# A hybrid streaming encoder step: key loads spread over the query tiles, and split weights kept in DRAM for the second token group

## The chip, the cores and the metric

The kernel runs on one core of one Trainium2 chip. The metric is the device time of one execution in microseconds (us); the figure for the kernel before is the median of three runs. A profile is one more execution, with the hardware profiler on. Names of engines: TensorE (PE in the rows; PEld is its weight load), VectorE (DVE), ScalarE (ACT), GpSimd (POOL), SyncE (SP). A name with a q at its end (SPq, ACTq, POOLq) is the engine's queue of instructions, where it issues DMAs.

## The reference, cut to what matters

One layer: RMSNorm, one input projection to `[q | k | v | z_a | forget | B | C | h_c | z_c]`, forgetting attention (8 heads of 64) beside a short gated convolution, one output projection, residual, final norm. 16 meta tokens and 2048 prompt tokens make 2064 positions; 128 sample tokens (8 streams of 16, each with 256 cached rows) go through the same weights.

```python
h = rmsnorm(xp, norm_g[l])
q, k, v, za, logf, bg, u, zc = project(h, w_in[l], b_f[l])     # p = h @ w_in, 1024 x 4104
o_a = fox_prompt_attention(q, k, v, logf)                      # softmax(q.k/8 + c_t - c_s, causal) @ v
y_c = bg * causal_conv(u_full, conv_w[l])
cat = concat([o_a * silu(za), y_c * silu(zc)])
xp = xp + cat @ w_out[l]
```

All values are float32. The matrix engine gets each operand as two halves: `h` is the value rounded to the short format (F32R), `l` the difference, and a product is `h*h + l*h + h*l`, three matmuls.

## The kernel before

**Token groups.** The positions are worked through in two groups (`GROUPS`, line 39): the first has 1280 positions and the 128 sample tokens, 1408 columns in four tiles (256, 384, 384, 384); the second has the other 784, in tiles of 256, 256 and 272. Each group goes through norm, values of heads 0 to 3, then keys, queries and gates of the four pairs of heads woven with attention, then the convolutions. Between the groups stand the sample attention and the splitting of the output weights `w_out` (`split_out`), woven with the first group's convolutions; the output projection comes last.

**Weights.** A block of input weights is 1024 x 128, `raw`, [128, 8, 128] in float32, 0.52 MB, read in pieces of 512 bytes. `weight_order` (line 535) lists the 30 blocks of one group, twice. Two of the 30 make up the values of heads 4 to 7; 28 are split singly, 56 in both groups. `fetch_w` (line 465) issues the load of the next block on ScalarE's queue into the one buffer `raw`; `split_w` (line 474) copies it to `wh` on ScalarE, subtracts on VectorE into `wl`, and fetches the next. `wh` and `wl` have two buffers each. `load_w` (line 517) hands a block to its user and splits the one after it. `project` (line 544) does the matmuls: per token tile 8 x 3 of them into one PSUM tile `ps`, of which there are two. `split_wv` (line 492) does the same for 256 columns of values, with the subtraction on GpSimd (`wvh`, `wvl`); for heads 0 to 3 the forget columns are added (`raw8`).

**What a projection leaves.** Keys and queries are split (`eh`, `el`, two buffers each) and stored on GpSimd's queue (`STORES`, line 1563) to DRAM: `kh_d`, `kl_d`, `qh_d`, `ql_d`, for sample tokens `sqk_d`; gates and convolution results from `kf` (two buffers) to `gz_d` and `cat_d`.

**Attention.** A unit is 256 queries of one head (272 in the last), two or three score tiles: 5 units a head in the first group, 3 (7 tiles) in the second. `scores_of` (line 966) loads, scores and exponentiates; `weights_of` transposes and splits the weights (`tp`, `ph`, `pl`); `values_of` multiplies with the values `vb` (one buffer, loaded per head). `load_head` (line 905) loads a head's keys into one of two sets of buffers: two halves for `ka`, the upper half once more for `kb` (64 rows of up to 2064 positions, 0.53 MB each in the second group), and the sums of the forget gates. `load_queries` does the like for a unit (`qa`, `qb`). All of this is issued on SP. At each unit `scores_of` first loads the keys of the next head, if they are not yet asked for, then the queries of the next unit:

```python
            for ahead in range(2):
                if loaded < H and loaded <= h + ahead and ("k", loaded // 2) in ready:
                    self.load_head(ph, loaded)
                    loaded += 1
                if asked < len(units) and asked <= n + ahead and ("q", units[asked][0] // 2) in ready:
                    self.load_queries(ph, asked, st)
```

**Order.** The program order is made by a planner (`Times`, line 68): it estimates when each instruction could run, `weave` (line 215) takes the next piece from the first stream that could go on, and `settle` (line 235) fixes the order on VectorE, ScalarE, GpSimd and SP by the estimated times. TensorE runs in the order in which the pieces were taken. Every engine works in its order: an instruction that waits holds up all behind it.

Where a helper records every operation, all instructions have one line, 278; the rows are told apart by their tiles.

## Time and profile before

| | |
|---|---|
| median of three runs (lowest to highest) | 1661.03 us (1653.34 to 1663.23) |
| the profiled execution | 1664.7 us |
| its span, first to last instruction | 1662.9 us |
| TensorE busy | 1537.2 us, 92% |
| VectorE, ScalarE, GpSimd busy | 862.4, 630.8, 479.1 us |
| read from and written to DRAM | 137.28 MB, 66.93 MB |

Busy times leave out instructions that issue DMAs, and the end of a matmul is modelled, so that TensorE's busy time is no measure of how well it is used; its idle time is what the order of the work leaves open. The granted clock (PEclk) is 1.00 where TensorE ran at 2.4 GHz throughout and 0.50 where it ran at 1.2 GHz.

### The profile page before, as it was taken

What the parts mean: (1) busy time and instruction counts of PE and PEld (TensorE: products, weight loads), DVE (VectorE), ACT (ScalarE), POOL (GpSimd) and SP (SyncE); (2) the same over time, 40 slices, a digit from 0 to 9 for tenths busy, and PEclk for the clock granted to TensorE, in tenths of its full rate; (3) what the DMA queues carried; (4) which work ended last, traced back from release to release, by engine and by line L of the source; (5) the groups of instructions that cost most, each with busy time, mean ns of one, the idle gap of its engine ahead of it and who ended that gap; (6) DMA issues with size and microseconds to landing.
All of it is one profiled execution on the core that took longest, in us unless ns stands there. A gap on an engine that the chain in (4) does not pass through costs nothing.

```text
span 1662.9 us, 27715 instructions
## 1 busy us (share of the span) xinstructions
PE 1537.2 (92%) x10311; PEld 1449.2 (87%) x10311; DVE 862.4 (52%) x2276; ACT 630.8 (38%) x1196; POOL 479.1 (29%) x750
## 2 busy tenths in 40 slices
PE   5779999999899999899996899999999999999996
PEld 4779999999899987898995888999998999878885
DVE  4525657426666657472231656767776775212221
ACT  4314545325454243231111455555654554111221
POOL 2542435533211321124231223212211112223332
PEclk9899999999999998999997899999999999999998
DMA  7446554365532576433227453355644231364442
GB/s 194 119 122 156 149 130 122 111 160 141 134 89 57 166 224 217 151 74 78 52 69 155 106 140 105 98 133 126 185 84 112 49 86 34 86 234 146 134 141 87
DMA packets 159143, 206.06 MB, mean 124 GB/s; under 512 B 22220, under 2 KB 123108, under 8 KB 156320
## 3 DMA queue, kind: packets, MB, share of 16 engines
q1 hardware_dynamic: 73952, 106.38, 22.3%
q10 hardware_dynamic: 61360, 30.94, 12.0%
q0 software_dynamic: 23696, 66.96, 11.6%
q8 instruction: 82, 1.34, 0.3%
q14 instruction: 53, 0.43, 0.1%
HBM read 137.28 MB, written 66.93 MB: 123 GB/s over the span
## 4 chain that ended last, share of the span: by engine, by line
PE 67%; DMA 15%; issue 8%; DVE 4%; POOL 3%; ACT 2%; SPq 1%; ACTq 0%; POOLq 0%; DVEq 0%
PE ps L278 43%; PE sp L278 9%; PE o L278 8%; PE tp L278 6%; DMA raw<-in_w_in_dram 3%; DMA cat_d<-kf 2%; DMA sqk_d<-el 2%; DMA vn<-in_cache_v_dram 2%; SPq L278 1%; PE tr L278 1%; DMA qb<-ql_d 1%; DMA kb<-kh_d 1%; DMA o_d<-ol 1%; DMA kb<-c_d 1%; DVE wl L278 1%
## 5 line engine op out<-in xcount | busy, mean ns | idle before, releaser
L278 PE MATMUL ps<-hh,wh 128*128 128x256 f32 (+2 forms) x1568 | 502.7, 321 | 22.4 <-DVE el L278 11.6
L278 PE MATMUL ps<-hl,wh 128*128 128x256 f32 (+2 forms) x1568 | 486.2, 310 | 0.0
L278 PE MATMUL ps<-hh,wl 128*128 128x256 f32 (+2 forms) x1568 | 485.3, 310 | 0.0
L278 PEld LDWEIGHTS ps<-hh,wh 128*128 128x128 f32 x1568 | 302.7, 193 | 31.2 <-DVE el L278 12.2
L278 PEld LDWEIGHTS ps<-hl,wh 128*128 128x128 f32 x1568 | 302.7, 193 | 1.4
L278 PEld LDWEIGHTS ps<-hh,wl 128*128 128x128 f32 x1568 | 301.6, 192 | 0.0
L278 ACT CAST ph<-tp 128x512 fp32r<-128x512 f32 (+2 forms) x360 | 169.9, 488 | 196.8 <-PE tp L278 175.3
L278 DVE TENSOR_TENSOR pl<-tp,ph 128x512 fp32r<-128x512 f32 (+2 forms) x360 | 197.3, 564 | 88.8 <-ACT ph L278 84.4
L278 DVE TENSOR_SCALAR_CACHE_REDUCE s<-sp 128x384 f32<-128x384 f32 (+3 forms) x360 | 211.0, 599 | 37.7 <-PE sp L278 36.4
L278 ACT ACTIVATE s<-s,nm 128x128 f32<-128x128 f32 (+16 forms) x136 | 170.5, 1254 | 72.6 <-DVE nm L278 72.2
L278 PE MATMUL tp<-ident,s 128*128 128x128 f32 (+1 forms) x1224 | 174.9, 267 | 9.7 <-DVE pl L278 8.8
L278 PE MATMUL o<-ph,vb 128*128 128x256 f32 (+4 forms) x584 | 167.5, 306 | 3.2 <-DMA vb<-v_d 2.7
L278 PE MATMUL sp<-kb,qb 68*128 68x384 f32 (+3 forms) x360 | 143.9, 400 | 22.3 <-DVE s L278 12.1
L278 PEld LDWEIGHTS tp<-ident,s 128*128 128x128 f32 (+1 forms) x1224 | 142.4, 143 | 14.4 <-DVE pl L278 10.0
L278 PE MATMUL o<-pl,vb 128*128 128x256 f32 (+4 forms) x584 | 151.4, 285 | 0.1
L278 PE MATMUL sp<-ka,qa 128*128 128x384 f32 (+3 forms) x360 | 133.7, 371 | 0.0
L278 POOL TENSOR_TENSOR gz<-gz,otmp 64x256 f32<-64x256 f32 (+1 forms) x64 | 47.3, 739 | 255.7 <-DVE otmp L278 244.0
L278 PE MATMUL ps<-o,ch 128*128 128x512 f32 x374 | 118.5, 396 | 0.9 <-DMA o<-o_d 0.7
L278 PEld LDWEIGHTS o<-ph,vb 128*128 128x128 f32 (+1 forms) x584 | 111.2, 190 | 6.7 <-DMA vb<-v_d 3.2
L278 PEld LDWEIGHTS o<-pl,vb 128*128 128x128 f32 (+1 forms) x584 | 111.9, 192 | 1.4 <-DVE pl L278 0.4
L278 DVE TENSOR_TENSOR wl<-raw,wh 128x1024 fp32r<-128x1024 f32 x56 | 69.6, 1243 | 59.0 <-ACT wh L278 58.8
L278 PE MATMUL ps<-wvh,hh 128*128 128x272 f32 (+3 forms) x288 | 87.2, 303 | 5.0 <-ACT sv L278 4.6
(218 smaller groups left out, 2292.2 us busy)
## 6 DMA issues: line engine op xcount, KB each, us to landing
raw<-in_w_in_dram ACTq DMA_DIRECT2D x59, 512.0 KB
cr<-cat_d SPq DMA_DIRECT2D x17, 512.0 KB
v_d<-vv POOLq DMA_DIRECT2D x32, 256.0 KB, 2.7
vb<-v_d SPq DMA_DIRECT2D x8, 1024.0 KB
oxt<-in_x_prompt_dram SPq DMA_DIRECT2D x16, 512.0 KB
out_dram<-oxt POOLq DMA_DIRECT2D x16, 512.0 KB, 3.0
xt<-in_x_prompt_dram SPq DMA_DIRECT2D x15, 512.0 KB
qa<-qh_d SPq DMA_DIRECT2D x112, 64.0 KB
```

The costliest lines, as they stand in the source:

```text
L278: r = f(*a, **k)
```

## The change

`load_head` no longer issues the loads of a head's keys but returns them as four parts. `scores_of` issues one part with each score tile, and all that are left before the head that needs them begins. The first token group stores `wh` and `wl` of each block to DRAM when it has split them (`wh` by ScalarE's queue, `wl` by GpSimd's), and those of the values too; the second group loads them from there on SP, in place of loading and splitting the block again.

```diff
     def fetch_w(self, queue="scalar"):
         n0 = next(self.worder, None)
         if n0 is None:
             return None
+        if n0 in self.w_d:
+            if n0 == OFF_V + 256:
+                next(self.worder)
+            return n0, None
         raw = self.wp.tile([P, NC, P], F32, name="raw")
 ...
         if OFF_V <= n0 < OFF_V + 512:
-            return n0, *self.split_wv(1, lambda k: self.wraw[1], then=self.next_w)
+            halves = self.split_wv(1, lambda k: self.wraw[1], then=raw is not None and self.next_w)
+            if raw is None:
+                self.next_w()
+            return n0, *halves
         wh = self.wp.tile([P, NC, P], F32R, name="wh", bufs=2)
         wl = self.wp.tile([P, NC, P], F32R, name="wl", bufs=2)
-        nc.scalar.copy(out=wh, in_=raw)
-        getattr(nc, W_E).tensor_tensor(out=wl, in0=raw, in1=wh.bitcast(F32), op=ALU.subtract)
+        if raw is None:
+            self.dma(out=wh, in_=self.w_d[n0][0])
+            self.dma(out=wl, in_=self.w_d[n0][1])
+        else:
+            nc.scalar.copy(out=wh, in_=raw)
+            getattr(nc, W_E).tensor_tensor(out=wl, in0=raw, in1=wh.bitcast(F32), op=ALU.subtract)
+            self.w_d[n0] = self.dram.tile([2, P, NC, P], F32R, name=f"w_d{n0}")
+            self.dma(out=self.w_d[n0][0], in_=wh, by="scalar")
+            self.dma(out=self.w_d[n0][1], in_=wl)
         self.wraw = self.fetch_w()
         return n0, wh, wl
 ...
+        if OFF_V + 256 * q in self.w_d:
+            dh, dl = self.w_d[OFF_V + 256 * q]
+            n = 272 if q == 0 else 256
+            for k in range(2):
+                sl = slice(4 * k, 4 * k + 4)
+                self.dma(out=wh[:, sl, :n], in_=dh[:, sl, :n])
+                self.dma(out=wl[:, sl], in_=dl[:, sl])
+            return wh, wl
 ...
+        self.w_d[OFF_V + 256 * q] = dh, dl = [self.dram.tile([P, NC, n], F32R, name=f"wv_d{q}{n}") for n in (272, 256)]
+        self.dma(out=dh[:, :, :272 if q == 0 else 256], in_=wh[:, :, :272 if q == 0 else 256])
+        self.dma(out=dl, in_=wl)
         return wh, wl
 ...
     def load_head(self, ph, h):
-        dma(out=ka[0:DH, :npos], in_=self.kh_d[p][rows, :npos])
-        dma(out=ka[DH:P, :npos], in_=self.kl_d[p][rows, :npos])
-        dma(out=kb[BR:, :npos], in_=self.kh_d[p][rows, :npos])
-        self.sums_rows(kb[2:4], h, 0, self.nk)
+        return [lambda: dma(out=ka[0:DH, :npos], in_=self.kh_d[p][rows, :npos]),
+                lambda: dma(out=ka[DH:P, :npos], in_=self.kl_d[p][rows, :npos]),
+                lambda: dma(out=kb[BR:, :npos], in_=self.kh_d[p][rows, :npos]),
+                lambda: self.sums_rows(kb[2:4], h, 0, self.nk)]
 ...
+            while parts and parts[0][0] <= h:
+                parts.pop(0)[1]()
             for ahead in range(2):
                 if loaded < H and loaded <= h + ahead and ("k", loaded // 2) in ready:
-                    self.load_head(ph, loaded)
+                    parts += [(loaded, f) for f in self.load_head(ph, loaded)]
                     loaded += 1
+                while parts and parts[0][0] <= h:
+                    parts.pop(0)[1]()
 ...
                 st["tiles"] += 1
+                if parts:
+                    parts.pop(0)[1]()
 ...
-        self.vp, fp, rp = self.open(gv, "vp1"), self.open(gf, "fp1"), self.open(xx, "rp1")
+        self.vp, fp = self.open(gv, "vp1"), self.open(gf, "fp1")
 ...
-        gate, v0 = stream(self.forget(1, fp)), stream(self.first_values(1, ready, self.split_wv(0, raws, fp)))
+        gate, v0 = stream(self.forget(1, fp)), stream(self.first_values(1, ready, self.split_wv(0, None)))
```

## Rows read from the trace of the kernel before

**Rows 1.** Stages: busy PE, PEld, DVE, ACT, POOL; granted clock, DMA share, GB/s.

```profile
0.00:40.00 40.00, 19.43 (x122) 18.27 (x123) 19.04 (x36) 17.60 (x28) 11.92 (x20) 1.00 0.74 193
...
120.00:560.00 440.00, 423.64 (x2937) 416.61 (x2936) 255.01 (x768) 196.29 (x406) 143.92 (x238) 0.97 0.48 122
560.00:700.00 140.00, 129.93 (x782) 118.68 (x782) 80.63 (x175) 43.01 (x86) 36.77 (x87) 0.95 0.67 216
...
860.00:940.00 80.00, 56.12 (x360) 52.81 (x359) 26.51 (x59) 18.36 (x35) 22.85 (x35) 0.81 0.60 134
940.00:1455.00 515.00, 499.24 (x3877) 478.47 (x3876) 333.04 (x923) 260.70 (x478) 116.75 (x179) 0.99 0.42 103
```

**Rows 2.** DMA queues (q10 ScalarE's, q0 GpSimd's): packets, MB, share of 16 engines.

```profile
q10 hardware_dynamic: 61360, 30.94, 12.0%
q0 software_dynamic: 23696, 66.96, 11.6%
```

**Rows 3.** Instructions of tile raw: count, ns least/median/most, first and last start.

```profile
L278 ACTq DMA_DIRECT2D raw<-in_w_in_dram x59: 374/374/444, 32.4 to 1433.0; - x59
L278 ACT CAST wh<-raw x56: 1033/1049/1083, 29.5 to 1441.9; 128x1024 fp32r<-128x1024 f32 x56
L278 DVE TENSOR_TENSOR wl<-raw,wh x56: 1205/1225/2055, 30.6 to 1443.0; 128x1024 fp32r<-128x1024 f32 x56
```

**Rows 4.** Timeline of PE, DVE, ACT, 893 to 917: start, us, instruction, [idle before, releaser].

```profile
916.39 0.79 PE L278 MATMUL sp<-kb,qb 68*128 68x512 f32 x1 [11.71 <-DVE s L278]
...
914.64 1.23 DVE L278 TENSOR_TENSOR wl<-raw,wh 128x1024 fp32r<-128x1024 f32 x1 [15.68 <-ACT wh L278]
...
893.87 0.37 ACTq L278 DMA_DIRECT2D raw<-in_w_in_dram  x1
...
913.56 1.04 ACT L278 CAST wh<-raw 128x1024 fp32r<-128x1024 f32 x1 [15.49 <-DMA raw<-in_w_in_dram]
```

**Rows 5.** Timeline of SP: first and last of six key loads.

```profile
891.47 0.50 SPq L278 DMA_DIRECT2D ka<-kh_d  x1
...
896.66 0.51 SPq L278 DMA_DIRECT2D kb<-kh_d  x1
```

**Rows 6.** Chain (first row), then timelines of ACT, PE, DVE, PE.

```profile
1084.93 11.36 DMA kb<-kh_d
...
1096.78 0.67 ACT L278 CAST ph<-tp 128x272 fp32r<-128x272 f32 x2 [4.17 <-DMA kb<-kh_d]
...
1097.69 0.46 PE L278 MATMUL tp<-ident,s 128*128 128x128 f32 x3 [2.36 <-DVE pl L278]
...
1274.03 1.22 DVE L278 TENSOR_TENSOR wl<-raw,wh 128x1024 fp32r<-128x1024 f32 x1
...
1275.66 0.46 PE L278 MATMUL tp<-ident,s 128*128 128x128 f32 x3 [1.95 <-DVE pl L278]
```

**Rows 7.** Timeline of PE: waits for queries in the first group.

```profile
192.84 0.35 PE L278 MATMUL sp<-kb,qb 68*128 68x256 f32 x1 [2.71 <-DMA qb<-ql_d]
...
421.85 0.55 PE L278 MATMUL sp<-kb,qb 68*128 68x256 f32 x1 [4.47 <-DMA qb<-ql_d]
```

**Rows 8.** Chain (start, us, what) and timeline of PE: waits for el.

```profile
103.24 15.35 DMA sqk_d<-el
...
119.32 0.69 PE L278 MATMUL ps<-hh,wh 128*128 128x384 f32 x1 [8.14 <-DVE el L278]
...
336.14 10.73 DMA sqk_d<-el
...
347.60 0.60 PE L278 MATMUL ps<-hh,wh 128*128 128x384 f32 x1 [3.45 <-DVE el L278]
```

**Rows 9.** Chain: loads, and matmuls of a block in the second group.

```profile
243.13 4.84 DMA vb<-v_d
...
1144.68 1.44 PE ps L278 x12
...
1422.42 8.23 DMA raw<-in_w_in_dram
```

More of the change, by code (lines that the diff above doesn't have):

```diff
@@ L344, in setup @@
         const = self.open(ctx, "const")
-        dram = self.open(ctx, "dram", space=DRAM)
+        dram = self.dram = self.open(ctx, "dram", space=DRAM)
+        self.w_d = {}
         self.acc, self.sps, self.ops, self.tps, self.trp = (self.open(ctx, n, space=PSUM)
@@ L969, in scores_of @@
         units = st["units"]
-        loaded, asked = 0, 0
+        loaded, asked, parts = 0, 0, []
         while ph not in self.summed:
@@ L1511, in run @@
         xx.close()
-        self.vp, fp, rp = self.open(gv, "vp1"), self.open(gf, "fp1"), self.open(xx, "rp1")
-        def raws(k):
-            raw = rp.tile([P, NC, P], F32, name="raw", bufs=RPB)
-            self.dma(out=raw, in_=self.w_v[:, :, OFF_V + P * k:OFF_V + P * k + P])
-            return raw
+        self.vp, fp = self.open(gv, "vp1"), self.open(gf, "fp1")
         ready = set()
-        gate, v0 = stream(self.forget(1, fp)), stream(self.first_values(1, ready, self.split_wv(0, raws, fp)))
-        xx.close()
+        gate, v0 = stream(self.forget(1, fp)), stream(self.first_values(1, ready, self.split_wv(0, None)))
         self.nc.step(gate)
```

## The prediction

> **What bounds the kernel now.** I read the busy times by stage first, then the waits of TensorE in its timeline, then what each waited for on the other engines, and last the chain and the DMA queues. The stages [rows 1] show a kernel that TensorE fills: 423.64 of 440 us from 120 to 560, 499.24 of 515 us from 940 to 1455. The matmuls are the same after the change, so only TensorE's idle time can be won or lost, with the slower clock behind it. It is 20.6 us in the first 40 us, 16.4 from 120 to 560, 10.1 from 560 to 700, 23.9 from 860 to 940 (where the second token group begins, granted clock 0.81 on average), and 15.8 from 940 to 1455. The largest wait of the second group is 11.71 us before the matmul at 916.39, for VectorE's eviction of a score [rows 4]. VectorE had stood 15.68 us before `wl<-raw,wh`; that one stood behind ScalarE's `wh<-raw`, which had stood 15.49 us for a `raw` load issued at 893.87. In-order engines thus turned one late weight load into a stall of the scores, which don't need that weight. The load was late because from 891.47 to 896.66 SP issued the key loads of two heads [rows 5], six of 0.53 MB.
>
> **The change, part by part.** The sum is made against the profiled execution, 1664.7 us (span 1662.9 and 1.8 around it); the median of the runs is 1661.03, so 3.7 us come off at the end.
>
> *Second group, weights: what goes.* Before, each of 56 weight blocks costs a load of 0.52 MB, 1049 ns on ScalarE, 1225 ns on VectorE and an issue of 374 ns on ScalarE's queue [rows 3]. The second group's 28 lose all of it: ScalarE 28 x (1.05 + 0.37) = 40 us, VectorE 28 x 1.225 = 34 us. Neither engine is the bound (VectorE 333 of 515 us from 940 to 1455 [rows 1]), so this counts only where TensorE stood behind it.
> (A) The stall at 904 to 916: VectorE no longer has the subtraction in its order, and the burst shrinks from 6 x 0.53 + 0.52 = 3.7 MB to 3 x 0.53 + 1.05 = 2.6 MB, as one head's keys move away. Bounds: 0 gain, if TensorE then waits for the weights themselves, and 11.71 plus what the clock gives back. The clock stood at its lower level for much of 860 to 940 (0.81 on average [rows 1], which is two fifths of 80 us at half speed), so some 2 to 4 us of it belong to this stall. I take 11 + 2 = 13, near the upper end, because the named cause is removed and not only shortened.
> (B) ScalarE's issue of `raw` also waits. From 1084.93 a key load took 11.36 us; the next ScalarE instruction behind the issue had stood 4.17 us with that load as releaser, and TensorE 2.36 us for `pl`; the wait of 1.95 us at 1275.66 has the subtraction just before it on VectorE [rows 6]. These two are 4.3 us; both the issue and the subtraction go, and key loads are spread. Bounds 0 and 12 (of 15.8 idle). I take 6: the two and the slower clock behind them.
>
> *Keys one part with each query tile.* `load_head` returns its four parts. Head h+1's parts go out with the first four score tiles of head h (10 tiles per head in the first group, 7 in the second), what is left at the latest before head h+1. SP issues the same DMAs; what moves is that the queries of the next unit stand ahead of most key parts, not behind all of them. The loads come a whole head early, so lateness of a few tiles is covered by the other tiles of that head; with this cover gone a part would cost its landing, 5 to 11 us.
> (C) In the first group TensorE waits three times for parts of `qb` (the first and the last are [rows 7]), 9.2 us together, each some us after a head's keys were issued. Bounds 0 and 12 with the clock. I take 7. Before the first head nothing can be spread, its parts go at once.
>
> *First group: what is added.* Each of 28 blocks now also stores `wh` by ScalarE's queue and `wl` by POOL's, 0.52 MB each, and the two value blocks store 4.3 MB in all: 28 x 1.05 + 4.3 = 33.6 MB. The nearest row is POOL's queue: 66.96 MB in 11.6% of 1662.9 us, 2.88 us of the 16 engines for a MB [rows 2]; so 97 us of DMA time in some 860 us, 11 points on a share of 0.48 to 0.74 [rows 1]. ScalarE's added issue, 28 x 0.37 = 10 us, is hidden: it is busy 196 of 440 us. What stands behind a `wl` store on POOL's queue, if VectorE is late, are the stores of `el`, `eh` and `kf` and the gate products.
> (D) The stores that follow it on the engines. At 119.32 and 347.60 TensorE had waited 8.14 and 3.45 us for `el`, whose buffer was held by an `el` store that landed 15.35 and 10.73 us after its issue [rows 8]. 15.35 - 8.14 = 7.2 and 10.73 - 3.45 = 7.3: an `el` store that needs over about 7.2 us is paid by TensorE one for one. Both follow a weight split by a few us, so both get 1.05 MB more beside them, 1.05 x 2.88 = 3.0 us. Bounds: 0 (the stores come after), and all 8 K and Q blocks of the group at 3.0 plus 1.5 for the clock, 36. I take the two that are late already, 6.
> (E) In the first 40 us the share is 0.74 and 20.6 us are idle; four more MB there are 12 us of DMA time. Bounds 0 and 10. I take 2, since what is late there mostly waits for buffers and the three-engine chain of the norm.
> (F) From 560 to 700 (samples, splitting of w_out; 216 GB/s, share 0.67) five blocks add 15 us of DMA time against 10.1 us idle. Bounds 0 and 10; I take 3.
>
> *Second group, weights: what comes.* Two loads per block on SP, 1.05 MB in rows of 4 KB instead of 0.52 MB in pieces of 512 bytes. ScalarE's queue spent 12.0% of 1662.9 us on its 59, 3.4 us of the 16 engines each; the pair at 2.88 us a MB is 3.0 [rows 2]. So DMA time in this group is even.
> (G) Prefetch is shorter: the pair waits on SP for its buffer, that is for the end of the block before the one running, while `raw` was fetched one block further ahead. Behind it on SP stand queries, keys, `gz` and values, for which TensorE waits. A running block has 72 matmuls, 12 in 1.44 us: 8.6 us, more where attention is woven in. The nearest loads [rows 9]: 0.66 MB of `vb` in 4.84 us, 0.52 MB of `raw` in 8.23. The pair lies between 4.84 and 4.84 x 1.05/0.66 = 7.7 us or 8.2: within a block, just. Bounds 0 and 8 (four blocks that run alone after 864, 2 us each). I take 1.
> The Trainium skill, page "DMA: Bandwidth & Descriptors", section "Anatomy of one DMA", fits a DMA as 2.0 us plus its bytes at 436 GB/s: an estimate of 4.4 us for the pair, with which G would be 0 and the sum 1 us lower; the 8.23 us of a load half that size speak against using it here.
> The values' halves come in four loads on SP instead of two raws, ScalarE and POOL. The convolutions' matmuls cover that: nothing taken, 6 us if the cover fails.
>
> Sum: -13 - 6 - 7 + 6 + 2 + 3 + 1 = -14. 1664.7 - 14 = 1650.7; on the median 1647.
>
> **Rivals.** (1) *The stores decide, slower.* Every K and Q block of the first group, 8 of them, gets an `el` store over the 7.2 us of D: 8 x 4.5 = 36, while the gains reach 26 - 7 = 19, since query loads suffer in the same traffic: +17, 1661 + 17 = 1678. It decides if `el` stores near weight splits land in 10 us and more throughout; for it speak the two that do already, against it that the other stores of `el` in the group do not stop TensorE now. The Trainium skill, same page, section "Issuing engines are not separate DMA queues", says that DMAs of ScalarE, SP and POOL interleave on the same 16 engines; by this rule the store on ScalarE's queue is no cheaper than one on POOL's, and the late `raw` of [rows 4], on a queue of its own, agrees.
> (2) *The wait only moves.* After 904 TensorE waits for the next weight pair or for queries behind it on SP. A falls to 3 and G rises to 4: -14 + 10 + 3 = -1, 1660. For it: SP's issues of 891 to 897 stand in one file, and blocks run alone there. Against: the second load group is 1.1 MB smaller.
> (3) *More than the named waits go.* VectorE and ScalarE work in the shortest paths (score, exponential, transpose) from 940 to 1455, and with 34 and 40 us less in their order all 12 of B come, A gives 15, C 10, and the first group's stores cost 6: -31, 1630.
> That the change does not do what it says, keys unspread, could be where K is ready only just in time; head changes of the second group issue keys a head early, so only the first heads are affected.
>
> **Numbers.** Forecast 0.46, on its own 1635 to 1660; rival 1 0.23, rival 2 0.16, rival 3 0.15. A measurement of this kernel tells about 1% from no change, 1644.4 to 1677.6. Half the forecast's chance lies under it (0.23) and all of rival 3: faster 0.38. The other half, rival 2 and 0.03 of rival 1: same 0.42. The rest of rival 1: slower 0.20. The range takes rival 3 and half of rival 1: 1626 to 1678.
>
> **What would show it.** `wh` and `wl` splits counted 28, not 56, VectorE some 34 us lower. A right: no wait of over 4 us between 895 and 935 and the clock of that stage above 0.9; wrong: TensorE's wait there names `wh`, `wl` or `qb`. B: no ScalarE wait on a key load after 940. C: waits for `qb` in 120 to 560 under 3 us in sum. D: the two waits for `el` grow to about 11 and 6.5; if there are five or more, rival 1 holds. F: idle from 560 to 700 about 13. The forecast fails above all if idle time before 860 grows by over 20 us.

## The result, and the profile after

| | before | after |
|---|---|---|
| median | 1656.51 us (1649.52 to 1663.23, 6 runs) | 1640.22 us (1632.28 to 1641.51, 6 runs) |
| ratio to before, 95% interval | | 0.9888 [0.9852, 0.9924] |
| profiled execution, span | 1664.7, 1662.9 us | 1641.5, 1639.7 us |
| TensorE, VectorE, ScalarE, GpSimd busy | 1537.2, 862.4, 630.8, 479.1 us | 1530.2, 823.3, 603.4, 485.6 us |
| read from and written to DRAM | 137.28, 66.93 MB | 154.09, 100.55 MB |

The change takes 1.1% off. The stages of after, in the columns of [rows 1] (the last one ends 20 us earlier than there, since the kernel ends 23 us earlier):

```profile
0.00:40.00 40.00, 19.29 (x128) 17.94 (x128) 15.71 (x32) 15.43 (x25) 13.59 (x23) 1.00 0.85 252
120.00:560.00 440.00, 408.22 (x2757) 399.29 (x2757) 236.80 (x722) 186.63 (x388) 150.35 (x252) 0.95 0.54 155
560.00:700.00 140.00, 127.31 (x812) 119.53 (x811) 82.32 (x189) 43.87 (x88) 37.21 (x87) 0.95 0.66 207
860.00:940.00 80.00, 74.49 (x507) 72.31 (x506) 22.99 (x59) 11.95 (x26) 25.83 (x40) 0.94 0.60 187
940.00:1435.00 495.00, 494.66 (x3910) 476.56 (x3909) 312.81 (x915) 244.10 (x463) 111.11 (x179) 1.00 0.44 136
```

Two things happened at once. In the second group TensorE has almost no idle time left (0.3 of 495 us, where [rows 1] had 15.8 of 515), and the stretch around 900 us is 74.49 of 80 us busy in place of 56.12. In the first group it lost: 408.22 us busy of 440 in place of 423.64, with 2757 matmuls done in place of 2937, so that the kernel falls behind there. The clock stage by stage tells the same: 0.81 became 0.94, but 0.97 became 0.95.

The splits of a block, by groups of instructions (busy us, mean ns, then idle before), and the DMA queues and issues (queues: packets, MB, share; issues: KB each, median us to landing where known), beside [rows 2, 3]:

```profile
L278 DVE TENSOR_TENSOR wl<-raw,wh 128x1024 fp32r<-128x1024 f32 x28 | 34.2, 1222 | 23.2 <-ACT wh L278 23.1
L278 ACT CAST wh<-raw 128x1024 fp32r<-128x1024 f32 x28 | 29.4, 1050 | 56.7 <-PE ps L278 39.6 <-DMA raw<-in_w_in_dram 17.1
```

```profile
q0 software_dynamic: 28432, 85.90, 14.6%
q10 hardware_dynamic: 34192, 29.89, 8.5%
...
w_d<-wh ACTq DMA_DIRECT2D x28, 512.0 KB
w_d<-wl POOLq DMA_DIRECT2D x28, 512.0 KB, 8.7
wh<-w_d SPq DMA_DIRECT2D x28, 512.0 KB
wl<-w_d SPq DMA_DIRECT2D x28, 512.0 KB
```

So the change does what it says: 28 splits in place of 56, VectorE 39.1 us and ScalarE 27.4 us less busy.

What TensorE waited for (us in total, times, longest), first from 120 to 560 us, with the values' waits of before in the last line; then from 860 to 950 us of after:

```profile
PE o L278 <- DMA vb<-v_d: 9.7, 4, 2.7
PE tr L278 <- ACT kf L278: 9.4, 1, 9.4
PE sp L278 <- issue: 3.7, 1, 3.7
PE ps L278 <- DVE el L278: 3.4, 1, 3.4
...
PE o L278 <- DMA vb<-v_d: 2.7, 2, 2.3
```

```profile
PE sp L278 <- DMA qb<-ql_d: 4.2, 1, 4.2
PE ps L278 <- DVE el L278: 1.3, 1, 1.3
```

The wait of 11.71 us of [rows 4] is gone; 4.2 us for queries stand in its place. The waits for queries of the first group [rows 7] are gone too. The waits for values grew there from 2.7 to 9.7 us, and one of 9.4 us for `kf` is new. Its cause is in the chain (start, us, what) and in ScalarE's timeline, in that order:

```profile
146.31 15.61 DMA gz_d<-kf
```

```profile
162.00 0.37 ACT L278 COPY kf<-ps 128x256 f32<-128x256 f32 x1 [11.36 <-DMA gz_d<-kf]
```

A store of a gate on GpSimd's queue took 15.61 us and held one of the two `kf` buffers; ScalarE, which works in order, stood 11.36 us before the next `kf`.

### The profile page after: what moved, and what is told of

Its sections match the earlier page's. It is cut to its first block, busy times and chain, and to the rows that moved or that the text cites. A ratio compares the mean times of both kernels' runs of the same rounds, so it can differ in the third digit from the quotient of the medians.

```text
span 1639.7 us, 27851 instructions
## 1 busy us (share of the span) xinstructions
PE 1530.2 (93%) x10311; PEld 1444.4 (88%) x10311; DVE 823.3 (50%) x2246; ACT 603.4 (37%) x1164; POOL 485.6 (30%) x778
## 3 DMA queue, kind: packets, MB, share of 16 engines
HBM read 154.09 MB, written 100.55 MB: 155 GB/s over the span
## 4 chain that ended last, share of the span: by engine, by line
PE 76%; DMA 12%; issue 5%; POOL 3%; ACT 1%; DVE 1%; SPq 0%; ACTq 0%; POOLq 0%; DVEq 0%
PE ps L278 48%; PE sp L278 11%; PE o L278 9%; PE tp L278 7%; DMA vb<-v_d 2%; PE tr L278 2%; DMA raw<-in_w_in_dram 1%; DMA oraw<-in_w_out_dram 1%; DMA qh_d<-eh 1%; DMA gz_d<-kf 1%; DMA cat_d<-gz 1%; DMA out_dram<-sv 1%; DMA vo<-vs_d 1%; DMA c_d<-ones 1%; DMA qb<-ql_d 1%
## 5 line engine op out<-in xcount | busy, mean ns | idle before, releaser
L278 PE MATMUL ps<-hh,wh 128*128 128x256 f32 (+2 forms) x1568 | 502.0, 320 | 25.3 <-DVE kf L278 12.3
L278 PE MATMUL o<-pl,vb 128*128 128x256 f32 (+4 forms) x584 | 150.4, 284 | 0.0
L278 PEld LDWEIGHTS o<-ph,vb 128*128 128x128 f32 (+1 forms) x584 | 111.7, 191 | 13.4 <-DMA vb<-v_d 10.7
L278 PEld LDWEIGHTS ps<-o,ch 128*128 128x128 f32 x374 | 70.1, 188 | 20.6 <-DMA o<-o_d 5.0
```

What stands on the lines that cost most here:

```text
L278: r = f(*a, **k)
```

## The experiments

To compare them, one cut of the program by its matmuls, in us of each profiled execution. The columns: up to the first score mask; up to the last score mask of the first group; up to the transposes of the second group's norm; up to the 272-column tile of the second group's first key block; from there to its first score mask (the group change); up to the first output matmul; the rest.

| kernel | start | attention 1 | samples | conv., norm | group change | second group | rest | span |
|---|---|---|---|---|---|---|---|---|
| before | 136.2 | 403.3 | 158.5 | 168.6 | 50.8 | 537.8 | 207.7 | 1662.9 |
| after | 143.0 | 428.6 | 160.2 | 165.0 | 32.7 | 507.3 | 202.9 | 1639.7 |
| e1_keys | 135.4 | 386.9 | 148.8 | 175.1 | 52.2 | 510.4 | 209.3 | 1618.1 |
| e2_weights | 144.5 | 435.2 | 185.1 | 153.2 | 32.2 | 512.3 | 202.7 | 1665.2 |
| e3_stores | 139.3 | 433.2 | 187.0 | 138.8 | 50.5 | 540.5 | 202.8 | 1692.1 |
| e4_loads | 128.5 | 410.5 | 158.7 | 168.7 | 32.7 | 515.6 | 208.6 | 1623.3 |
| f1_queries | 138.2 | 385.1 | 158.2 | 168.9 | 52.2 | 529.6 | 207.9 | 1640.1 |
| f2_pool | 136.4 | 390.4 | 147.2 | 176.3 | 51.3 | 549.7 | 208.2 | 1659.5 |
| f3_wh | 141.6 | 409.8 | 161.6 | 168.3 | 51.2 | 538.9 | 207.9 | 1679.3 |
| f4_wl | 142.3 | 422.5 | 164.1 | 169.8 | 51.0 | 538.4 | 202.3 | 1690.3 |
| g2_four | 140.4 | 402.4 | 150.4 | 187.6 | 28.8 | 521.1 | 208.3 | 1639.0 |
| g3_both | 129.7 | 393.3 | 148.4 | 176.5 | 36.1 | 508.7 | 208.6 | 1601.3 |
| g4_pieces | 137.0 | 403.1 | 157.8 | 169.1 | 30.9 | 518.8 | 209.0 | 1625.7 |
| h1_copy | 136.6 | 388.4 | 149.0 | 209.2 | 31.6 | 510.2 | 209.2 | 1634.2 |

Each row is one execution. The runs of before lie between 1649.52 and 1672.16 us, and its profiled execution took 1664.7; that of f1_queries, 1642.0, is the fastest of its eight. So a difference of a few us between two rows shows nothing by itself, and the gains against the row of before are some us too large; what a kernel is worth is told by its median and its ratio to before, run beside it.

Against before, after loses 6.8 + 25.3 + 1.7 - 3.6 = 30 us ahead of the group change and gains 18.1 + 30.5 = 48.6 behind it, and 4.8 in the rest: 23 us between the two profiled executions, 16 between the medians.

### The four parts by themselves

The theory at first was that the weights decide: their loading wins most, their stores cost most, the keys matter little. The rival: the keys decide.

*e1_keys*: the kernel before with the keys' parts spread; weights as before. The edit is the `load_head` and `scores_of` part of the change's diff, alone.

> The kernel before with the keys' parts one with each score tile, weights as before. Theory (the weights decide: their splitting held up the second group, their stores cost the first): 0 to -6 us; the second group's first block starts within 5 us of 867, and the wait of about 12 us before a score near 910 stays at 6 us or more, since the subtraction is still in VectorE's order. Rival (the bunched keys were the cause of the second group's stalls, and the spread parts beside the values' load cost the first group): -15 to -25 us, the wait near 910 under 3 us, and new waits for vb of some 2 us each, about 8 us in sum, in the first group.

1622.42 us, 0.9761 [0.9709, 0.9813] (the ratio to before, with its 95% interval): faster than the changed kernel. The keys decide, as the rival has it: 16.4 us in the first group's attention and 27.4 in the second group. But the gain of some 40 us is beyond the rival's 15 to 25, and one of its signs failed: the wait near 910 is not under 3 us but 12.43 (at 897.40, shown below), as the theory had it.

*e2_weights*: the whole change, but the keys' loads bunched as before.

```diff
-        return [lambda: dma(out=ka[0:DH, :npos], in_=self.kh_d[p][rows, :npos]),
-                lambda: dma(out=ka[DH:P, :npos], in_=self.kl_d[p][rows, :npos]),
+        dma(out=ka[0:DH, :npos], in_=self.kh_d[p][rows, :npos])
+        dma(out=ka[DH:P, :npos], in_=self.kl_d[p][rows, :npos])
...
-                    parts += [(loaded, f) for f in self.load_head(ph, loaded)]
+                    self.load_head(ph, loaded)
```

> The changed kernel with the keys' loads bunched as before. Theory (the weights decide): -10 to -18 us, nearly the whole change; idle time of TensorE from the first score of the second group to the output under 5 us, the first group some 25 to 30 us longer than before. Rival (keys): 0 to -5 us, a wait of 5 us or more at the second group's first scores, the first group under 10 us longer.

1667.72 us, 1.0045 [1.0015, 1.0074]. The weights' part of the change alone is slower than before; both expectations had a gain. It does gain 18.6 us at the group change and 25.5 in the second group, and loses 31.9 in the first group's attention and 26.6 in the samples, of which the next stage gives 15.4 back. One wait for queries at 161.30 us lasted 16.15 us.

*e3_stores*: the kernel before, with all the stores of split weights in the first group, and nobody loads them.

```diff
+        if n0 not in self.w_d:
+            self.w_d[n0] = self.dram.tile([2, P, NC, P], F32R, name=f"w_d{n0}")
+            self.dma(out=self.w_d[n0][0], in_=wh, by="scalar")
+            self.dma(out=self.w_d[n0][1], in_=wl)
```

> The kernel before with all stores of split weights in the first group, but nobody loads them: the second group splits again, keys as before. Theory (DMA traffic and queue places of the stores cost the first group): +25 to +35 us, all of it before the second group's first block, with waits for el, kf and query loads grown. Rival (the first group grew for the spread keys or for the planner's other order): 0 to +8 us.

1696.44 us, 1.0206 [1.0152, 1.0259], as the theory expected. What TensorE waited for from 120 to 560 us, and behind the dots its waits for queries in before:

```profile
PE sp L278 <- DMA qb<-ql_d: 16.2, 2, 9.0
PE o L278 <- DMA vb<-v_d: 6.2, 2, 5.9
PE o L278 <- ACT ph L278: 3.9, 1, 3.9
PE sp L278 <- DMA qb<-c_d: 3.7, 1, 3.7
PE ps L278 <- DVE el L278: 3.3, 1, 3.3
...
PE sp L278 <- DMA qb<-ql_d: 7.2, 2, 4.5
PE sp L278 <- DMA qb<-c_d: 2.0, 1, 2.0
```

The largest named growth is in loads: queries from 9.2 to 19.9 us and values from 2.7 to 6.2; the `el` buffers pay 3.3 us, not more than before. TensorE's idle time in the first group's attention grew from 16.4 to 38.3 us, so that about a third of the growth is in other, smaller waits (for `ph` and `kf` among them).

*e4_loads*: the kernel before with one stored block, which the second group loads as halves for each of its 28 single blocks.

```diff
+        if n0 in self.w_d:
+            return n0, None
...
+            if not self.w_d:
+                self.one = self.dram.tile([2, P, NC, P], F32R, name="w_d")
...
+            self.w_d[n0] = self.one
```

> The kernel before with no stores but one: the halves of the first key block go to DRAM, and the second group loads these for every one of its 28 blocks; so its projections are made with one block's weights. Keys and the values of heads 0 to 3 as before. Theory (the weights decide): -40 to -50 us, all of it after the second group's first block, which starts within 5 us of 867. Rival (keys, or shorter prefetch on SP eats the gain): -5 to -20 us.

1623.95 us, 0.9756 [0.9691, 0.9822]. The loads win 18.1 us at the group change and 22.2 behind it. So three large terms stand behind a small result: keys -40, loads -40, stores +34 us (1659 times the ratios less one). They don't simply add; g3_both below shows where keys and loads overlap. And e2_weights, loads and stores without the keys, is 7 us slower than before, where -40 and +34 would make it 6 faster: with the loads in place the stores cost more than by themselves (44 us, by g3_both).

### Is it the queue's order or the bunch?

*f1_queries*: the keys stay one bunch, but the next unit's queries are issued ahead of them.

```diff
-                if loaded < H and loaded <= h + ahead and ("k", loaded // 2) in ready:
-                    self.load_head(ph, loaded)
-                    loaded += 1
                 if asked < len(units) and asked <= n + ahead and ("q", units[asked][0] // 2) in ready:
                     self.load_queries(ph, asked, st)
                     asked += 1
+                if loaded < H and loaded <= h + ahead and ("k", loaded // 2) in ready:
+                    self.load_head(ph, loaded)
+                    loaded += 1
```

> The kernel before with one edit: at each unit the queries of the next unit are issued ahead of the next head's keys, which still go out as one bunch. Order theory: the keys cost time because the queries stand behind three to four key loads on SP, so that their place in the queue is what the spreading wins. Then most of the 20 us that spreading the keys won ahead of the second group's first block comes here too, and part of the 27 us of the second group: 15 to 35 us faster than before, waits for qb from 120 to 560 under 3 us in sum. Rival, burst theory: what costs is 1.1 to 1.6 MB of key loads at one time on the 16 DMA engines, beside weight loads and stores, whoever is in front. Then 0 to 6 us, with qb waits still there or turned into waits for weights and values.

1649.11 us, 0.9926 [0.9903, 0.9949], a gain of 12 us, under the 15 to 35 of the order theory and over the 0 to 6 of the burst theory. In the profiled execution, 7 us under that median, the first group's attention takes 385.1 us, as short as with spread keys (386.9): there the order alone does as much. The second group gains 8.2 us of the 27.4: there the bunch counts. In the columns of [rows 1]: attention 1, group change and second group of before, then attention 1 of f1_queries, then the second group of e1_keys:

```profile
136.20:539.50 403.30, 386.94 (x2699) 380.31 (x2698) 239.54 (x734) 186.97 (x390) 136.44 (x224) 0.97 0.47 122
...
866.60:917.40 50.80, 30.33 (x205) 29.01 (x205) 10.26 (x17) 6.41 (x13) 13.09 (x22) 0.80 0.67 149
917.40:1455.20 537.80, 518.71 (x3980) 496.16 (x3979) 345.19 (x961) 270.48 (x496) 121.73 (x187) 0.98 0.42 104
```

```profile
138.20:523.30 385.10, 377.24 (x2693) 370.73 (x2692) 238.84 (x734) 186.63 (x390) 136.57 (x224) 1.00 0.49 127
```

```profile
898.40:1408.80 510.40, 505.81 (x3980) 487.20 (x3979) 345.38 (x961) 270.86 (x495) 122.80 (x187) 1.00 0.44 108
```

In the first group TensorE's idle time falls from 403.30 - 386.94 = 16.4 to 7.9 us, and its busy time by 9.7 us for nearly the same matmuls, as the granted clock rises from 0.97 to 1.00. In the second group the same 3980 matmuls take 12.9 us less, beside 14.5 us less idle time. In these two stages the clock gives back about as much as the waits. At the group change it does not: there after has 15.0 us less idle time than before and 3.1 us less busy time, for nearly the same matmuls.

### What makes the group change slow

In e1_keys that stretch is as slow as before. ScalarE, then VectorE, then TensorE there:

```profile
870.28 1.04 ACT L278 CAST wh<-raw 128x1024 fp32r<-128x1024 f32 x1 [11.10 <-DMA raw<-in_w_in_dram]
873.68 0.37 ACTq L278 DMA_DIRECT2D raw<-in_w_in_dram  x1
894.57 1.04 ACT L278 CAST wh<-raw 128x1024 fp32r<-128x1024 f32 x1 [17.20 <-DMA raw<-in_w_in_dram]
```

```profile
895.64 1.23 DVE L278 TENSOR_TENSOR wl<-raw,wh 128x1024 fp32r<-128x1024 f32 x1 [17.41 <-ACT wh L278]
```

```profile
897.40 0.79 PE L278 MATMUL sp<-kb,qb 68*128 68x512 f32 x1 [12.43 <-DVE s L278]
```

It is [rows 4] again. A load of 0.52 MB issued at 873.68 was in use at 894.57, 20.9 us later.

*f2_pool*: e1_keys, with the second group's subtraction on GpSimd, so that VectorE's order no longer holds it.

```diff
-        getattr(nc, W_E).tensor_tensor(out=wl, in0=raw, in1=wh.bitcast(F32), op=ALU.subtract)
+        self.nsplit = getattr(self, "nsplit", 0) + 1
+        getattr(nc, W_E if self.nsplit <= 28 else "gpsimd").tensor_tensor(out=wl, in0=raw, in1=wh.bitcast(F32), op=ALU.subtract)
```

> The kernel before with the keys' loads spread (as in e1_keys), and in the second group the subtraction wl<-raw,wh on GpSimd in place of VectorE; no weights are stored. It tests step A's cause: in e1_keys the wait for VectorE's score eviction near 890 was still 12.4 us. If VectorE's order (the late subtraction ahead of the eviction) makes that wait, it is gone: from the second group's first block to its first score mask 36 to 42 us where e1_keys has 52, and the whole 1606 to 1614 us. Rival: the late raw load holds TensorE anyway, as the next block needs its halves: then TensorE waits there for wh or wl, 48 to 54 us in that stretch, and 1618 to 1628 in all. A third way, that GpSimd's subtraction (over 2 us where VectorE needs 1.2) delays its stores of el and eh: slower than e1_keys by over 5 us.

1661.4 us, 1.001 [0.9982, 1.0039]; the group change takes 51.3 us, as the rival expected, though the wait for VectorE's score eviction is down from 12.4 to 0.2 us. ScalarE's timeline:

```profile
866.20 1.05 ACT L278 CAST wh<-raw 128x1024 fp32r<-128x1024 f32 x1 [9.18 <-DMA raw<-in_w_in_dram]
867.57 0.63 ACT L278 ACTIVATE eh<-ps 128x256 fp32r<-128x256 f32 x2
...
884.08 1.05 ACT L278 CAST wh<-raw 128x1024 fp32r<-128x1024 f32 x1 [6.75 <-DMA raw<-in_w_in_dram]
885.03 0.39 ACT L278 ACTIVATE eh<-ps 128x272 fp32r<-128x272 f32 x1
```

The wait went one engine up: now ScalarE's evictions `eh` stand behind `wh<-raw`, and TensorE waits for `el` and `kf` in place of the score. VectorE's order was where it hurt; that the late load is what is wrong, the next run shows. Why the second group lost another 39 us against e1_keys is not settled. It is the third way of the expectation: a subtraction took 2.39 us on GpSimd for 1.23 on VectorE, and GpSimd, which issues the stores, was 178.67 us busy there in place of 122.80.

*g4_pieces*: the kernel before; `raw` is loaded and split as ever, but in the second group from one stored copy in rows of 4 KB.

```diff
-        getattr(self.nc, queue).dma_start(out=raw, in_=self.w_v[:, :, n0:n0 + P])
+        getattr(self.nc, queue).dma_start(out=raw, in_=self.one if n0 in self.seen_w else self.w_v[:, :, n0:n0 + P])
...
+        if self.one is None:
+            self.one = self.dram.tile([P, NC, P], F32, name="w_d")
+            self.dma(out=self.one, in_=raw)
+        self.seen_w.add(n0)
```

> The kernel before, whose second group still loads raw on ScalarE's queue and splits it on ScalarE and VectorE, but reads it from one stored copy of a block in rows of 4 KB in place of pieces of 512 bytes (so its 28 single blocks are projected with one block's weights). It tells what the second group wins by the stored halves: the splitting work off ScalarE and VectorE, or loads that don't arrive late. Pieces theory: the raw loads of 512-byte pieces land some 20 us after their issue beside the keys' loads of long rows, and with long rows they land in under 8 us: the waits of ScalarE for raw after 860 go, the stretch from the first block to the first score mask falls from 51 to 34 to 40 us, and the whole to 1622 to 1636, as in e4_loads. Splitting theory: the work and its order on the engines cost the time: 1648 to 1660, waits for wl or kf still there.

1631.9 us, 0.98 [0.9748, 0.9852], whose interval overlaps that of e4_loads, with all the splitting still on ScalarE and VectorE. Its group change and second group, and its late load:

```profile
867.00:897.90 30.90, 27.27 (x205) 25.97 (x204) 10.38 (x17) 6.52 (x13) 12.99 (x22) 0.95 0.78 219
897.90:1416.70 518.80, 509.11 (x3981) 488.74 (x3980) 344.51 (x961) 270.64 (x496) 120.78 (x187) 0.99 0.38 108
```

```profile
882.85 0.33 ACTq L278 DMA_DIRECT2D raw<-w_d  x1
894.06 1.04 ACT L278 CAST wh<-raw 128x1024 fp32r<-128x1024 f32 x1 [8.03 <-DMA raw<-w_d]
```

The group change is as short as with the halves (30.9 against 32.7 us), the second group 3 us longer than in e4_loads. The load comes 11.2 us after its issue, not in the under 8 that the pieces theory named. What the stored halves win is mostly that they come in long rows (33 of 40 us by the ratios), not that the engines split less. In this run, as in e4_loads, all blocks come from one stored copy; h1_copy below, which reads eleven different ones, shows the same short group change, so that it is not the one copy that does it there.

### What the stores cost

*f3_wh* and *f4_wl*: the kernel before, which stores only `wh` by ScalarE's queue, or only `wl` by GpSimd's (28 blocks, 14.7 MB each; the values' halves are not stored).

```diff
+        if n0 not in self.w_d:
+            self.w_d[n0] = self.dram.tile([P, NC, P], F32R, name=f"w_d{n0}")
+            self.dma(out=self.w_d[n0], in_=wh, by="scalar")
```

> The kernel before, whose first group stores only wh of its 28 single blocks (14.7 MB) by ScalarE's queue; nobody loads them, wl and the values' halves are not stored. All stores (33.6 MB) made the kernel before 38 us slower. Bytes theory: any 14.7 MB on the 16 DMA engines cost in proportion, here 13 to 20 us, as many as f4_wl. Order theory: what costs is the place on GpSimd's in-order queue, where a wl store that waits for VectorE holds back the stores of keys, queries and gates: here 0 to 6 us.

For f4_wl the last line is:

```diff
+            self.dma(out=self.w_d[n0], in_=wl)
```

> The same with wl alone (14.7 MB), by GpSimd's queue. Bytes theory: 13 to 20 us slower than before, like f3_wh. Order theory: 25 to 35 us slower, with the waits for el, kf and loads of what GpSimd's queue stores.

1681.03 us, 1.0122 [1.0096, 1.0149], and 1690.87 us, 1.0171 [1.0135, 1.0207]. Both cost, 20 and 28 us (by ratio), so neither queue is free. The same bytes cost 8 to 10 us more on GpSimd's queue: the two ran beside the same runs of before, and the slowest run of f3_wh (1682.21) is below the fastest of f4_wl (1685.19). So f3_wh came out at the upper end of what the bytes theory gives, and f4_wl inside what the order theory gives; neither theory has both. The sum, 48 us, is more than what e3_stores paid for all 33.6 MB, so the price does not go by bytes alone.

*g2_four*: e1_keys, with the halves of only four blocks stored and loaded, those behind the late loads of the group change (4.2 MB).

```diff
+            if n0 in (OFF_Q, OFF_ZA, OFF_K + P, OFF_Q + P):
+                self.w_d[n0] = self.dram.tile([2, P, NC, P], F32R, name=f"w_d{n0}")
+                self.dma(out=self.w_d[n0][0], in_=wh, by="scalar")
+                self.dma(out=self.w_d[n0][1], in_=wl)
```

> The kernel before with the keys' loads spread (as in e1_keys), and of the split weights only four blocks (queries and gate of the first pair of heads, keys and queries of the second) stored by the first group and loaded by the second: 4.2 MB in place of 33.6. These are the blocks whose late raw loads made the waits of 12.4 and 7.5 us near the second group's first block in e1_keys. If they alone are what the stored weights win there, that stretch falls from 52 to 34 to 40 us, the stores cost 3 to 8 us by the price of 38 us for 33.6 MB, and the kernel takes 8 to 14 us less than e1_keys: 0.967 to 0.972 of before. Rival: the lateness moves on to the blocks behind these four, or the stores near the start weigh more than their share: 0.974 to 0.982.

1640.51 us, 0.9845 [0.9788, 0.9902]: slower than e1_keys, and than both expectations. The group change fell to 28.8 us, even under the 34 to 40 expected, but start and attention took 5.0 and 15.5 us more than in e1_keys for 4.2 MB of stores, and convolutions and norm 12.5 (8.8 of them in one wait for `kf`, whose buffer a store of `cat_d` held; why, is not settled). One block is stored near 40 us, the other three between 92.94 and 148 us, where the first heads' loads start. The chain there (start, us, what), then SP's timeline:

```profile
122.09 13.27 DMA raw<-in_w_in_dram
```

```profile
123.48 0.50 SPq L278 DMA_DIRECT2D ka<-kl_d  x1
135.38 0.56 SPq L278 DMA_DIRECT2D kb<-kh_d  x1
```

SP stood 11.4 us before a key load, until a weight load that ScalarE had issued came in; the scores then waited for queries behind it on SP.

*g3_both*: e1_keys and e4_loads together, that is the change without its stores.

> The kernel before with the keys' loads spread and the second group's weights loaded as halves (as in e4_loads, from one stored block, so that the second group's 28 single blocks are projected with one block's weights); no stores but that block. This is the change without its stores. Alone, the keys took 36 us off and the loads 37. If both draw on the same idle time of the second group (from its first block to the output 563, 562 and 548 us with the keys alone, the weights alone, both), it takes 1600 to 1608, some 55 us under before and 35 to 40 under the changed kernel: the two sum to 73 less the 15 to 20 counted twice. If they were independent: 1583 to 1590. If the stores were not what separates the changed kernel from this one: above 1620.

1603.11 us, 0.9623 [0.9577, 0.9669], inside the 1600 to 1608 that were expected. Keys and loads draw on the same idle time of the second group (510.4, 515.6 and together 508.7 us) and do not add there. The stores are what mainly separates this kernel from the changed one: 0.9888 less 0.9623, 44 us. (The values' halves, which the change also loads, are split again here.)

*h1_copy*: e1_keys; while SP has nothing to issue, it copies eleven unsplit weight blocks within DRAM into rows of 4 KB, and the second group loads those.

```diff
+    def copy_w(self, blocks):
+        for n0 in blocks:
+            self.w_d[n0] = self.dram.tile([P, NC, P], F32, name=f"w_d{n0}")
+            self.nc.sync.dma_start(out=self.w_d[n0], in_=self.w_v[:, :, n0:n0 + P])
...
+        self.copy_w([n0 for n0 in self.weight_order()[1:14] if not OFF_V <= n0 < OFF_V + 512])
```

> The kernel before with the keys' loads spread (as in e1_keys); nothing of the split weights is stored. Instead, when the second group's norm is done, SP issues eleven DMAs from DRAM to DRAM that copy eleven of the unsplit input weight blocks (those of queries, gates and keys behind the first block of keys) into rows of 4 KB (5.8 MB), in the stretch where SP issues nothing for some 150 us and the DMA engines are 0.2 to 0.3 busy; the second group loads these copies into raw on ScalarE's queue and splits them as before. Pieces theory (late raw loads in pieces of 512 bytes make the stall at the second group's first block): that stretch falls from 52 to 30 to 38 us and nothing is lost ahead of it: 0.964 to 0.970 of before, faster than the changed kernel by some 2%. Rival: the copies are slow (each piece read and written by itself) and still run when the keys and queries are loaded, or hold the convolutions' raw loads: 0.974 to 0.985, with waits for raw or qb after 840.

1638.72 us, 0.9894 [0.9856, 0.9932], slower than even the rival's 0.974 to 0.985. The group change fell from 52.2 to 31.6 us and the second group kept its 510, but convolutions and norm grew from 175.1 to 209.2. SP, ScalarE and TensorE there:

```profile
693.32 46.08 SPq L278 DMA_DIRECT2D w_d<-in_w_in_dram  x10
```

```profile
723.68 0.38 ACTq L278 DMA_DIRECT2D raw<-in_w_in_dram  x1
724.09 0.48 ACT L278 COPY u<-ps 128x384 f32<-128x384 f32 x1 [31.14 <-DMA w_d<-in_w_in_dram]
```

```profile
725.84 1.21 PE L278 MATMUL sp<-ident,xt 16*128 16x16 f32 x8 [26.38 <-DVE hl L278]
```

ScalarE stood 31.14 us before its next weight load until a copy of SP's was done, and TensorE 26.38 us behind it. The theory held for the group change, and the rival's cause, slow copies, for the rest; a version with the copies spread was not run. The best kernel that computes everything stays e1_keys, 0.9761 against the change's 0.9888.

## Why the prediction was right or wrong

The forecast of 1647 us was 7 us from the median, on the right side, by a sum whose terms were wrong and cancelled: +4 before the group change (C, D, E, F) where +30 was measured, and -18 from there on (A, B, G) where -48.6 was. The directions of the two parts were right; that their sum came out as near is luck.

**A, the stall: right that it goes, too small, and the cause one step short.** Taken 13, measured 18.1 us. The clock of the stretch is above 0.9 as said (0.94), and one wait is left over the 4 us that the prediction named, of 4.2 us at 926.80; it names queries, which the prediction gave as a sign of A being wrong, so a small part of rival 2 came true. TensorE's idle time there fell from 20.5 to 5.5 us, since waits for `kf` went with the one that was named. The step named the late load and the burst of keys ahead of it, but counted on VectorE's subtraction being gone. f2_pool took only that away, and the stretch stayed at 51.3 us; g4_pieces left it and brought the load in time, and the stall was gone. The step also credited the burst's shrinking by one head's keys; e1_keys, which has that, kept a stall of 12.43 us.

**B, second group: the step that failed in the gains.** Taken 6, bounds 0 and 12, measured 30.5. The bound was made from the 15.8 us of idle time, with the clock as a remainder; but the same matmuls, 518.71 us in before (shown at f1_queries), took 12 us less in after, at a clock of 0.99 for 0.98, which no wait shows:

```profile
929.50:1436.80 507.30, 506.96 (x3981) 487.88 (x3980) 319.27 (x938) 248.42 (x470) 115.76 (x185) 0.99 0.45 139
```

And B took only the waits that could be named (4.3 us), where all of them went. That no ScalarE instruction waits for a key load after 940 came true. Nor did B see that either part of the change does it nearly alone: e1_keys gets 27.4 of it with all weights split as before, e4_loads 22.2 with the keys bunched.

**C, the keys: right in kind, under half in size.** Taken 7, bounds 0 and 12; e1_keys has 16.4 and f1_queries 18.2 us. The waits for queries that step C summed are all gone in after. Again the clock was the missing half: 8.5 us of idle time and 9.7 of busy time in f1_queries. In the changed kernel the gain does not show, as the stores spend it in the same stage.

**D, E, F, the stores: the step that failed in the costs.** Taken 11; e3_stores has 34 us, and the whole change pays 44 against g3_both. D looked for the victims among the `el` stores, as those had been late in [rows 8]. Those waits did not grow to 11 and 6.5 (6.5 and 3.4 us in after, for 8.14 and 3.45). What paid in e3_stores were mostly the loads: queries 10.7 us more, values 3.5. In after it was values, 7.0 us more, and a gate store of 15.61 us that held a `kf` buffer: there D's mechanism, a buffer held by a late store on GpSimd's queue, came true on another tile. E, for the first 40 us, is nothing there (20.7 us idle for 20.6); the start as a whole lost 3.1 us in e3_stores and 6.8 in after. F, taken 3, is as good as nothing in e3_stores over both stages (325.8 us for 327.1). F's sign, idle time from 560 to 700 of about 13 us, is 12.7 in after. The rule behind rival 1, from the Trainium skill, page "DMA: Bandwidth & Descriptors", section "Issuing engines are not separate DMA queues", agrees with f3_wh, which costs 20 us though it adds nothing to GpSimd's queue. But what rival 1 made of it, that a store on ScalarE's queue is no cheaper, did not come out: f4_wl on GpSimd's costs 28.

**G and the values' four loads**: no wait for halves over 1 us stands in the second group after, so G's 1 us is not contradicted, and the cover held. The fit that G quotes from the Trainium skill, page "DMA: Bandwidth & Descriptors", section "Anatomy of one DMA", is stated there for DMAs that GpSimd issues, while the pair goes out on SP; the sum took nothing from it.

**Rivals.** Rival 1 had the price of the stores nearly right (36 us) by the wrong victims, and fell because the gains came to some 62 us (g3_both) where it granted 19. Rival 3 had the right direction in the second group, 27 us in A and B together where 48.6 was measured, but for the wrong reason: g4_pieces keeps the 34 and 40 us of splitting and still gets most of it. The sign named for failure, idle time before 860 up by over 20 us, did appear (69.5 to 91.9 us up to the group change); the forecast held only because the group change and the second group gave 30 us more than was thought.

## What to carry to other kernels

A wait on TensorE costs its length and can cost more in the clock behind it: here about as much again in the long stages of attention, a fifth at the group change. So size a gain by the stage's idle time and by what its matmuls take at full clock, not by the waits alone. Follow a late in-order instruction back to the transfer, and ask how that transfer is cut: a load in 512-byte pieces lost to its neighbours here, and moving the waiting instruction to another engine only moved the wait. Added stores were paid here by the loads nearest their deadlines and by one buffer that a late store held, and not where late stores had been seen before; even four blocks of them cost more than they gave back. So take a change with two parts apart before keeping both: here the small part alone beats the whole.

## What the runs showed of the hardware

**Pieces beside rows.** A `raw` of 0.52 MB in pieces of 512 bytes took 20.9 us from issue to use beside the keys' long rows (e1_keys), 11.2 us from a copy in rows of 4 KB (g4_pieces), and 8.23 us near the end of the second group of before [rows 9]. The Trainium skill, page "DMA: Bandwidth & Descriptors", section "Queues, rings and completion order", says that a DMA engine goes round its queues and takes a packet from each in turn. The three times would fit that, as a queue of short pieces would get fewer bytes a turn; that it is this, no run here shows by itself.

**A load holds another engine's load.** SP stood for a load that ScalarE had issued (g2_four), ScalarE for a copy of SP's (31.14 us, h1_copy) and, in before, for a key load [rows 6]. The traces show why. Every DMA that SP or ScalarE issues signals one of the same eight semaphores (counters that tell the engines what has landed; numbers 100, 101 and 104 to 109 in these traces), and is issued only when the last DMA that had this semaphore has landed; GpSimd's DMAs have eight others (111 to 118). In h1_copy SP's copies took 106 to 109, 100, 101 and 104 in turn. The one issued at 702.77 us had 109; its last update of 109 came at 723.58 us. ScalarE's `raw` has 109 too, and was issued at 723.68, with `u` and `hh` standing behind it; ScalarE had stood there since 693, that is from before that copy was issued, so the turns are fixed by the program and not by who comes first. In g2_four `kb<-kh_d` on SP shares 107 with ScalarE's `raw` of 122.09: its last update came at 135.36 us, and SP issued at 135.38. In before, `raw` at 1096.36 shares 108 with the key load of 1084.93.

So at most eight such DMAs are on their way, and a slow one can stop both issuing engines and all that ScalarE has to compute behind its issue. That a slow `raw` or a bunch of keys hurts queries in this way fits f1_queries and g2_four; it was not tested with another number of semaphores.

**Ten copies within DRAM** (of the eleven) of 0.52 MB in 512-byte pieces kept SP 46.08 us at their issue (h1_copy), while the DMA engines were 0.66 busy from 700 to 740.
